# A DRAM scratch for rotated queries and keys, laid out row by row instead of block by block

## The chip, the core and the metric

The kernel runs on one core of one Trainium2 chip. The metric is device time in microseconds (us) of that core, the median of several runs. A core has five engines that each work through their own list of instructions: TensorE (PE, matmuls, with weight loads shown as PEld), VectorE (DVE), ScalarE (ACT), GpSimd (POOL) and SyncE (SP, which here only issues transfers). Transfers between DRAM and the on-chip buffers are issued by SP and by ACT and are carried out by 16 DMA engines.

## The reference, cut to what matters

One decoder layer on 1024 positions and width 2048: RMS norm, one input projection to 6144 columns, then differential attention with eight heads beside a gated linear recurrence with eight blocks, a gate on each, one output projection, residual and a final norm. The part that the change touches is the scores of the attention:

```python
q = rope(q.reshape(bsz, seq, N_ATTN_HEADS, 2, QK_DIM), cos, sin)   # QK_DIM = 64
k = rope(k.reshape(bsz, seq, N_ATTN_HEADS, 2, QK_DIM), cos, sin)
...
s = jnp.einsum('bhmqd,bhmkd->bhmqk', qb, kb).astype(jnp.float32) * scale
mask = jnp.arange(end)[None, :] <= (s0 + jnp.arange(Q_BLOCK))[:, None]
p = jax.nn.softmax(jnp.where(mask, s, -jnp.inf), axis=-1)
w = p[:, :, 0] - lam * p[:, :, 1]
```

Each head has two score maps (m = 0, 1) with 64 query and 64 key channels each; rope turns the first 32 channels against the second 32.

## The kernel before, in words

Work goes in two passes over the sequence, `b` = 0 and 1, of 512 positions each. A pass has sixteen units in the order of the table `UNITS`: eight heads (four projections of 128 columns each) and eight recurrent blocks (two projections each). Then `outputs(b)` computes the output projection of these positions. A projection (`project`, its matmuls in `triple`, L368) is 48 matmuls of 512 columns: 16 blocks of 128 input rows, each as three products, because every operand is split in two parts of fewer bits, "hi" and "lo" (`split`, L170 the ACT cast to hi, L171 the subtraction to lo). The weights are streamed: SP loads 128x512 pieces (`load`, L156, which issues every SP load), ACT casts them, POOL subtracts, and TensorE uses them.

The order of instructions on every engine is fixed when the kernel is built. A scheduler of "slots" (`Slots`) advances by one tick with nearly every triple of matmuls. Side tasks (rope, values, recurrence, loading a head, scores, softmax weights, head output) are generators that `yield` a number of ticks, and each one's instructions stand in the lists of the engines where their tick falls. An engine waits at each instruction until the data are there. The tile framework hands out eight DMA semaphores, named DMAHW0 to DMAHW7 below, in turn to the transfers of both issuing engines, and a transfer whose turn comes waits until the last one on its semaphore has landed, where that isn't known yet.

The path that the change touches, for each head and pass:

- `head` multiplies the two q/k projections by cos and sin (DVE, L174). The 128 rows of each are four groups of 32: query m=0, query m=1, key m=0, key m=1. The first projection has the first 32 channels, the second the other 32.
- `rope` adds and subtracts, and splits the two results into four tiles of 128x512: `t2` and `t4` (hi of the first and of the second half), `t1` and `t3` (lo of both). ACT then stores the four tiles to the DRAM scratch `fs` (L471).
- `head_load` brings them back on SP in the form that the score matmuls need: for each m a key tile of 128 rows (hi first, hi second, lo first, lo second: 4 blocks of 32 rows), a query tile with the 64 hi rows twice, and one with the 64 lo rows twice. In the second pass the key tiles and values of the first pass are loaded as well (eight transfers from `fs` and two from `vs`). The loader starts a head once its stores were issued six ticks before.
- `score` runs at least 24 ticks (pass 0) or 28 ticks (pass 1) after the loads: L634 multiplies the first query tile with the key tile, L635 adds the product of the second query tile.
- `values` stores the value tiles of pass 0 to `vs` on ACT (L493), and `head_out` writes the head's output, with L723 on ACT and the matmuls L726 and L737.

Of the kernel before, what the change touches and what calls it, by code (L numbers as in the profile page):

```python
# [13 lines left out]
F32 = mybir.dt.float32  # L14
# [11 lines left out]
HALF = 512  # L26
# [81 lines left out]
class Trunk:  # L108
# [351 lines left out]
    def rope(self, b, h, ts):  # L460
        nc = self.nc
        t1, t2, t3, t4 = ts
        self.tt(t1.f, t1.f, t2.f, ALU.subtract)
        self.tt(t3.f, t3.f, t4.f, ALU.add)
        yield 1
        self.split(t1.f, t2, t1)
        self.split(t3.f, t4, t3)
        yield 4
        fs = self.dram.tile([4, 4, 32, HALF], F32, name=self.nm("fs"))
        for i, t in enumerate((t2, t4, t1, t3)):  # L470
            nc.scalar.dma_start(fs[:, i], t.f)  # L471
        self.rel(*ts)
        self.fs[h, b] = fs
        yield 6
        self.ready.add(("q", h, b))
# [109 lines left out]
    def head_load(self, h, l):  # L585
        k, q, v = [], [], []
        for c in range(l + 1):
            ks = []
            for m in range(2):
                kk = self.allocr()  # L590
                self.load(kk.f, self.fs[h, c][2 + m].rearrange("i r c -> (i r) c"))
                ks.append(kk)
            k.append(ks)
        for i in (0, 2):
            for m in range(2):
                t = self.allocr()
                src = self.fs[h, l][m, i:i + 2].rearrange("i r c -> (i r) c")
                self.load(t.f, src.unsqueeze(0).broadcast_to([2, 64, HALF]))
                q.append(t)
        if l:  # L600
            vs = []
            for d in self.vsc[h]:
                t = self.allocr()
                self.load(t.f, d)
                vs.append(t)
            v.append(vs)
        self.hd[h, l] = (k, q, v)
        self.loaded[h, l] = self.sl.now
# [331 lines left out]
```

## Time and profile before

| what | value |
|---|---|
| time, median of 3 runs | 2099.34 us (2096.14 to 2101.21) |
| the profiled execution's own time | 2100.45 us |
| its span, first to last instruction | 2098.7 us |
| TensorE busy | 1724.3 us, 82% of the span |
| ACT, POOL and DVE busy | 38%, 40% and 37% |
| mean granted TensorE clock | 0.913 of full speed |
| moved by DMA | 237.02 MB, mean 113 GB/s |

TensorE is the busiest engine by far, so what counts is where it stands still and where it runs at the lower of its two clocks. A matmul of 512 columns takes about 0.23 us at the full clock; the durations in the profile also hold the time in which a matmul stands in the pipeline behind another one.

### The profile page before, as it was taken

Reading aid. Unit: us, or ns where it says so; the run is one execution under the profiler, and the core shown is the slowest. Engines: PE = TensorE matmul, PEld = TensorE weight load, DVE = VectorE, ACT = ScalarE, POOL = GpSimd, SP = SyncE. Lnnn points to the kernel's source line nnn. Section 1 sums busy time; section 2 is a strip of 40 time slices with the busy share of each in tenths; the row PEclk is TensorE's granted clock in tenths of the full one; section 3 lists DMA queues with packets and bytes.
Section 4 is the critical chain, followed back from the end, with each engine's and each line's share of the span. In section 5 each row is a group of like instructions: output and inputs, shape, how many; then the busy total and the mean of one; then the engine's idle time right before and its main releaser. Section 6 shows DMA issues by size and latency. Waiting matters only on the chain.

```text
span 2098.7 us, 22044 instructions
## 1 busy us (share of the span) xinstructions
PE 1724.3 (82%) x7716; PEld 1408.4 (67%) x7716; DVE 779.1 (37%) x1333; ACT 804.7 (38%) x1393; POOL 849.8 (40%) x710
## 2 busy tenths in 40 slices
PE   7758868787786779989979787878787879799996
PEld 5646756566665667768867576767676767587885
DVE  8515342414151325741115242424252515265101
ACT  6215242525161236633414342525252424365321
POOL 7313433434342325765632242424233333266560
PEclk9879989898898889999989898989898999899998
DMA  5432333333323235423652242323233232255312
GB/s 209 135 112 74 109 97 110 94 105 93 120 79 120 79 98 170 159 81 99 214 185 84 79 119 81 113 90 113 91 106 97 90 115 83 89 181 188 113 63 80
DMA packets 131502, 237.02 MB, mean 113 GB/s; under 512 B 13248, under 2 KB 17472, under 8 KB 131392
## 3 DMA queue, kind: packets, MB, share of 16 engines
q1 hardware_dynamic: 116032, 206.27, 31.6%
q10 hardware_dynamic: 15360, 29.36, 4.0%
q8 instruction: 60, 0.98, 0.2%
q14 instruction: 50, 0.41, 0.1%
HBM read 197.83 MB, written 37.75 MB: 112 GB/s over the span
## 4 chain that ended last, share of the span: by engine, by line
PE 31%; DMA 14%; DVE 7%; ACT 3%; issue 2%; SPq 2%; POOL 1%; ACTq 0%; POOLq 0%; DVEq 0%
PE pq L368 11%; PE pq L829 8%; PE sw L829 8%; DMA fs<-b 5%; DMA b<-fs 4%; DMA b<-w_in 4%; SPq L156 2%; DVE b L174 2%; DMA ms<-b 1%; PE pq L758 1%; DVE sw L639 1%; ACT wide L646 1%; DVE b L533 1%; ACT b L170 1%; DVE wide L654 1%
## 5 line engine op out<-in xcount | busy, mean ns | idle before, releaser
L368 PE MATMUL pq<-b,b 128*128 128x512 f32 x4512 | 1151.6, 408 | 83.7 <-DVE b L171 64.0
L171 POOL TENSOR_TENSOR b<-b,b 128x512 fp32r<-128x512 f32 x504 | 671.9, 1347 | 1033.0 <-ACT b L170 720.8
L368 PEld LDWEIGHTS pq<-b,b 128*128 128x128 f32 x4512 | 871.5, 198 | 263.9 <-DVE b L171 67.8
L170 ACT CAST b<-b 128x512 fp32r<-128x512 f32 x592 | 349.2, 617 | 962.2 <-DMA b<-w_in 390.5
L829 PE MATMUL pq<-b,b 128*128 128x512 f32 x768 | 197.6, 393 | 4.4 <-DVE wide L174 4.4
L829 PE MATMUL sw<-b,b 128*128 128x512 f32 x768 | 197.0, 392 | 0.0
L174 DVE TENSOR_TENSOR b<-pq,b 128x512 f32<-128x512 f32 x113 | 74.8, 686 | 276.6 <-PE pq L368 180.9
L829 PEld LDWEIGHTS pq<-b,b 128*128 128x128 f32 x768 | 144.8, 189 | 35.8 <-DVE wide L174 4.8
L829 PEld LDWEIGHTS sw<-b,b 128*128 128x128 f32 x768 | 145.6, 190 | 30.6
L174 POOL TENSOR_TENSOR b<-b,b 128x512 f32<-128x512 f32 (+1 forms) x98 | 126.4, 1291 | 65.2 <-DVE b L740 29.0
L635 PE MATMUL sw<-b,b 128*128 128x512 f32 (+2 forms) x192 | 70.7, 377 | 83.8 <-DMA b<-fs 83.8
L646 ACT ACTIVATE wide<-sw,mx 128x128 f32<-128x128 f32 (+7 forms) x128 | 93.9, 737 | 88.0 <-DVE mx L642 50.1
L639 DVE CUSTOM_DVE_ANT_0 sw<-sw,mask 128x128 f32<-128x128 f32 (+7 forms) x128 | 95.2, 774 | 79.6 <-PE sw L635 79.6
L758 PE MATMUL pq<-ident,wide 128*128 128x128 f32 x288 | 56.0, 304 | 66.9 <-DVE wide L654 63.2
L634 PE MATMUL sw<-b,b 128*128 128x512 f32 (+2 forms) x192 | 69.4, 367 | 40.5 <-DMA b<-fs 33.2
L635 PEld LDWEIGHTS sw<-b,b 128*128 128x128 f32 x192 | 38.4, 200 | 94.3 <-DMA b<-fs 88.9
L171 DVE TENSOR_TENSOR b<-b,b 128x512 fp32r<-128x512 f32 x88 | 88.9, 1033 | 29.3 <-ACT b L170 26.0
L455 DVE SCALAR_TENSOR_TENSOR b<-b,b 128x512 f32<-128x512 f32 x32 | 31.1, 971 | 178.0 <-ACT b L453 178.0
L758 PEld LDWEIGHTS pq<-ident,wide 128*128 128x128 f32 x288 | 38.0, 154 | 85.9 <-DVE wide L654 73.0
L768 DVE TENSOR_TENSOR b<-pq,b 128x512 fp32r<-128x512 f32 (+1 forms) x80 | 50.9, 636 | 103.6 <-ACT b L767 96.7
L767 ACT CAST b<-pq 128x512 fp32r<-128x512 f32 (+1 forms) x80 | 43.2, 540 | 99.3 <-PE pq L758 89.7
L634 PEld LDWEIGHTS sw<-b,b 128*128 128x128 f32 x192 | 38.2, 199 | 49.2 <-issue 30.3
(130 smaller groups left out, 1345.8 us busy)
## 6 DMA issues: line engine op xcount, KB each, us to landing
b<-w_in SPq DMA_DIRECT2D x384, 256.0 KB
b<-w_out SPq DMA_DIRECT2D x128, 256.0 KB
b<-fs SPq DMA_DIRECT2D x112, 256.0 KB
fs<-b ACTq DMA_DIRECT2D x64, 256.0 KB
b<-xt SPq DMA_DIRECT2D x32, 256.0 KB
ms<-b ACTq DMA_DIRECT2D x32, 256.0 KB
b<-ms SPq DMA_DIRECT2D x32, 256.0 KB
wide<-x SPq DMA_DIRECT2D x20, 256.0 KB
```

Source lines behind the costliest of these rows:

```text
L170: self.nc.scalar.copy(hi.r, x)
L171: (eng or self.nc.vector).tensor_tensor(out=lo.r, in0=x, in1=hi.f, op=ALU.subtract)
L174: (eng or self.nc.vector).tensor_tensor(out=out, in0=a, in1=b, op=op)
L368: self.nc.tensor.matmul(acc, lhsT=x.r[:, s], rhs=y.r, start=kt == 0 and j == 0, stop=kt == KT - 1 and j == 2)
L634: nc.tensor.matmul(o, lhsT=q[m].r[:, qs], rhs=kk, start=True, stop=False)
L635: nc.tensor.matmul(o, lhsT=q[2 + m].r[:, qs], rhs=kk, start=False, stop=True)
L639: nc.vector.tensor_tensor_reduce(out=s, in0=s, in1=self.mask[:, 896 - off:896 - off + cols], scale=1.0, scalar=NEG, op0=ALU.add, op1=ALU.m ...
L646: nc.scalar.activation(p[:, :cols], self.swide[m][:, :cols], AF.Exp, scale=QK ** -0.5, bias=mx[:, m:m + 1], accum_out=sm[:, m:m + 1])
L758: nc.tensor.transpose(self.tr[:, c:c + P], ws[qi][:, kb * P:(kb + 1) * P], self.ident)
L767: nc.scalar.copy(wh.r[:, first:], self.tr[:, first:])
L768: nc.vector.tensor_tensor(out=wl.r[:, first:], in0=self.tr[:, first:], in1=wh.f[:, first:], op=ALU.subtract)
L829: nc.tensor.matmul(accs[t], lhsT=x.r[:, s], rhs=z.r, start=i == 0 and j == 0, stop=i == KT - 1 and j == 2)
```

## The change

The scratch `fs` of a head gets another layout. Before it was group, block, row: for each of the four groups of 32 rows, four blocks (hi first, hi second, lo first, lo second) of 32 rows, 64 KB each. Now it is group, row, block: each of the 128 rows has six places side by side, 2 KB each, for hi first, hi second, lo first, lo second, hi first, hi second. Two more stores of 64 rows fill places 4 and 5 for the query groups. A key tile is places 0 to 3 of 32 rows. The two query tiles are places 0 to 3 and places 2 to 5 of 32 rows: the first now multiplies hi with hi and lo with lo, the second lo with hi and hi with lo, which sum to the same four products.

```diff
-        fs = self.dram.tile([4, 4, 32, HALF], F32, name=self.nm("fs"))
+        fs = self.dram.tile([4, 32, 6, HALF], F32, name=self.nm("fs"))
         for i, t in enumerate((t2, t4, t1, t3)):
-            nc.scalar.dma_start(fs[:, i], t.f)
+            nc.scalar.dma_start(fs[:, :, i].rearrange("g r c -> (g r) c"), t.f)
+        for i, t in enumerate((t2, t4)):
+            nc.scalar.dma_start(fs[:2, :, 4 + i].rearrange("g r c -> (g r) c"), t.f[:64])
         self.rel(*ts)
...
                 kk = self.allocr()
-                self.load(kk.f, self.fs[h, c][2 + m].rearrange("i r c -> (i r) c"))
+                self.load(kk.f, self.fs[h, c][2 + m, :, :4])
...
         for i in (0, 2):
             for m in range(2):
                 t = self.allocr()
-                src = self.fs[h, l][m, i:i + 2].rearrange("i r c -> (i r) c")
-                self.load(t.f, src.unsqueeze(0).broadcast_to([2, 64, HALF]))
+                self.load(t.f, self.fs[h, l][m, :, i:i + 4])
                 q.append(t)
```

On ACT, at the third head of pass 0, the list holds these rows (fs is the scratch, b are tiles of 128x512, and the size is that of the side that is written; in brackets the semaphores waited for). Before:

```order
L170 CAST b_1377<-b_1376 128x512 [waits DVE_49]
L471 DMA fs_1637<-b_1375 4x32x512 [waits Activation_49]
L471 DMA fs_1637<-b_1377 4x32x512 [waits DMAHW4_49,Activation_49]
L471 DMA fs_1637<-b_1374 4x32x512 [waits DMAHW5_49,DVE_49]
L471 DMA fs_1637<-b_1376 4x32x512 [waits DMAHW7_49,DVE_49]
L170 CAST b_1867<-b_1741 128x512 [waits DMAHW4_49]
```

And in the changed kernel at the same place:

```order
L170 CAST b_1381<-b_1380 128x512 [waits DVE_49]
L471 DMA fs_1641<-b_1379 128x512 [waits Activation_49]
L471 DMA fs_1641<-b_1381 128x512 [waits DMAHW0_49,Activation_49]
L471 DMA fs_1641<-b_1378 128x512 [waits DMAHW1_49,DVE_49]
L471 DMA fs_1641<-b_1380 128x512 [waits DMAHW3_49,DVE_49]
L473 DMA fs_1641<-b_1379 64x512 [waits DMAHW4_49]
L473 DMA fs_1641<-b_1381 64x512 [waits DMAHW5_49]
L170 CAST b_1851<-b_1716 128x512 [waits DMAHW1_49]
```

The written side of a store was four groups of 32 rows and is now one run of 128 rows, and the two stores of 64 rows stand ahead of the next cast of a weight piece.

On SP the same head is loaded by these rows. Before (b_1675 and b_1677 are the hi queries, b_1671 and b_1673 the keys, b_1679 and b_1681 the lo queries):

```order
L156 DMA b_1874<-w_in 128x512 [waits DMAHW6_49,PE_49]
L156 DMA b_1675<-fs_1637 128x1x512 [waits DMAHW4_49,DMAHW3_49]
L156 DMA b_1677<-fs_1637 128x1x512 [waits DMAHW1_49]
L156 DMA b_1671<-fs_1637 128x512 [waits DMAHW7_49,DMAHW5_49,DMAHW2_49]
L156 DMA b_1673<-fs_1637 128x512
L156 DMA b_1679<-fs_1637 128x1x512
L156 DMA b_1681<-fs_1637 128x1x512
L156 DMA b_1852<-w_in 128x512 [waits DMAHW6_49,DVE_49]
```

And in the changed kernel (b_1677 and b_1679 are the keys, the other four the queries):

```order
L156 DMA b_1880<-w_in 128x512 [waits DMAHW2_49,PE_49]
L156 DMA b_1677<-fs_1641 128x1x512 [waits DMAHW6_49,DMAHW3_49,DMAHW7_49,DMAHW1_49,DMAHW0_49]
L156 DMA b_1679<-fs_1641 128x1x512
L156 DMA b_1681<-fs_1641 128x1x512
L156 DMA b_1683<-fs_1641 128x1x512
L156 DMA b_1685<-fs_1641 128x1x512 [waits DMAHW5_49,DMAHW4_49,DMAHW2_49]
L156 DMA b_1687<-fs_1641 128x1x512
L156 DMA b_1858<-w_in 128x512 [waits DVE_49]
```

The six loads keep their place between two weight loads; the keys now stand first, the first load waits for all four large stores instead of two, and the last two loads wait for the two new stores.

## Rows read from the trace of the kernel before

**Rows 1.** The page's first part, busy time, share of the span and instructions, and its slices of the granted TensorE clock.

```profile
PE 1724.3 (82%) x7716; PEld 1408.4 (67%) x7716; DVE 779.1 (37%) x1333; ACT 804.7 (38%) x1393; POOL 849.8 (40%) x710
PEclk9879989898898889999989898989898999899998
```

**Rows 2.** Who TensorE waited for over the whole span: line, releaser, us in total, times, longest.

```profile
PE sw L635 <- DMA b<-fs: 83.8, 17, 9.3
PE pq L368 <- DVE b L171: 64.0, 7, 12.3
PE pq L758 <- DVE wide L654: 63.2, 22, 5.4
PE pq L726 <- ACT b L723: 44.1, 3, 14.8
...
PE sw L634 <- DMA b<-fs: 33.2, 6, 8.8
...
PE pq L737 <- DVE hs L734: 8.7, 2, 7.8
...
PE sw L634 <- ACT wide L646: 7.2, 1, 7.2
```

**Rows 3.** TensorE in order of time around the first scores of a head of pass 0: start, duration, what, and in brackets the idle time before and its releaser.

```profile
349.10 11.85 PE L368 MATMUL pq<-b,b 128*128 128x512 f32 x51
365.13 0.55 PE L634 MATMUL sw<-b,b 128*128 128x256 f32 x1 [4.18 <-DMA b<-fs]
372.81 0.58 PE L635 MATMUL sw<-b,b 128*128 128x256 f32 x1 [7.13 <-DMA b<-fs]
...
377.96 0.58 PE L635 MATMUL sw<-b,b 128*128 128x256 f32 x1 [4.36 <-DMA b<-fs]
378.34 8.58 PE L368 MATMUL pq<-b,b 128*128 128x512 f32 x30
```

**Rows 4.** ACT in order of time around the same head; ACTq is its sequencer, which issues transfers.

```profile
338.60 0.53 ACTq L471 DMA_DIRECT2D fs<-b  x1
...
339.69 2.74 ACTq L471 DMA_DIRECT2D fs<-b  x3
348.40 0.62 ACT L170 CAST b<-b 128x512 fp32r<-128x512 f32 x1 [8.75 <-DMA fs<-b]
350.97 0.62 ACT L170 CAST b<-b 128x512 fp32r<-128x512 f32 x1 [1.94 <-DMA fs<-b]
...
378.63 1.14 ACT L170 CAST b<-b 128x512 fp32r<-128x512 f32 x2 [25.73 <-DMA b<-w_in]
```

**Rows 5.** SP's issues in order of time around the same head (a merged row lasts from the first issue to the end of the last).

```profile
341.45 0.33 SPq L156 DMA_DIRECT2D b<-w_in  x1
348.45 13.91 SPq L156 DMA_DIRECT2D b<-fs  x6
```

**Rows 6.** The chain that ended last, in order of time, around a head of pass 1.

```profile
1364.94 10.80 DMA fs<-b
...
1375.82 4.38 SPq L156
...
1382.01 20.58 DMA b<-fs
```

**Rows 7.** TensorE in order of time around the same head of pass 1.

```profile
1372.91 9.12 PE L368 MATMUL pq<-b,b 128*128 128x512 f32 x39
1392.03 7.34 PE L368 MATMUL pq<-b,b 128*128 128x512 f32 x24 [10.00 <-DVE b L171]
...
1402.63 0.80 PE L635 MATMUL sw<-b,b 128*128 128x512 f32 x1 [2.35 <-DMA b<-fs]
...
1403.65 7.97 PE L368 MATMUL pq<-b,b 128*128 128x512 f32 x30
```

**Rows 8.** ACT in order of time around the same head of pass 1.

```profile
1390.15 0.62 ACT L170 CAST b<-b 128x512 fp32r<-128x512 f32 x1 [17.33 <-DMA b<-w_in]
```

**Rows 9.** Two stretches of pass 1 in which transfers of fs alone are under way: the stretch, its length, busy time (and instructions) of PE, PEld, DVE, ACT and POOL, granted clock, mean busy share of the 16 DMA engines, GB/s.

```profile
1366.50:1373.00 6.50, 6.50 (x33) 5.39 (x32) 0.69 (x1) 2.56 (x5) 2.44 (x2) 1.00 0.25 88
1384.50:1388.50 4.00, 0.00 (x0) 0.00 (x0) 0.00 (x0) 0.00 (x0) 0.00 (x0) 0.59 0.13 50
```

**Rows 10.** DMA queues (q10 is ACT's: packets, MB, share of 16 engines' span) and the issues of ACT and those of fs on SP (number, KB each).

```profile
q10 hardware_dynamic: 15360, 29.36, 4.0%
...
b<-fs SPq DMA_DIRECT2D x112, 256.0 KB
fs<-b ACTq DMA_DIRECT2D x64, 256.0 KB
...
ms<-b ACTq DMA_DIRECT2D x32, 256.0 KB
...
vs<-b ACTq DMA_DIRECT2D x16, 256.0 KB
```

**Rows 11.** Two other transfers of 256 KB on the chain that ended last: a store of a 128x512 tile on ACT (pass 1) and a load of a 128x512 weight piece on SP.

```profile
1329.29 4.88 DMA ms<-b
...
1847.41 2.78 DMA b<-w_out
```

**Rows 12.** What SP's own queue waited for over the whole span.

```profile
SPq L156 <- PE pq L368: 355.2, 112, 20.8
...
SPq L156 <- DMA fs<-b: 187.8, 34, 10.4
```

## The prediction, made before the changed kernel was run

> **What bounds the kernel now.** I read the page's first part, then TensorE's waits, then one head in each pass in order of time on TensorE, ACT and SP. TensorE is busy for 82% of the span, no other engine for more than 40% [rows 1], so time is won only where TensorE stands still or is slowed. Its list of waits [rows 2] is led by the scratch: L635 and L634 wait 83.8 and 33.2 us for loads of fs. L368 "for DVE L171" (64.0 us) and L726 "for ACT L723" (44.1 us) don't name fs, so their cause has to be found.
>
> In pass 0 [rows 3], TensorE runs out at 349.10 + 11.85 = 360.95 us and then waits 4.18, 7.13 and 4.36 us, all for fs: 15.7 us in one head. ACT issued the four stores at 338.60 to 342.4 [rows 4]. Two casts that need the stored tiles' buffers go at 348.40 and 350.97: the stores land one by one, 2.6 us apart. The last queries release L635 at 372.81 and 377.96, so the query loads land 5.15 us apart. SP issues nothing but fs from 348.45 to 362.4 [rows 5], so weight loads are held as well, and ACT waits 25.73 us for one of them [rows 4].
>
> In pass 1 the same trip is on the chain that ended last [rows 6]: 10.80 us for a store, SP from 1375.82 on, 20.58 us for a load. TensorE stops at 1382.03 for 10.00 us [rows 7]. The releaser named is a DVE subtraction, but it needs ACT's cast, and ACT stood for 17.33 us behind a weight load in its own order [rows 8]. So these waits of L368 are the fs trip as well, by way of a weight piece that was stuck behind it. L726 waits for an ACT instruction that stands in the same place (three of about 15 us). Behind that L635 still waits 2.35 us for fs.
>
> **Why the trip is slow.** While stores of fs alone are under way, a quarter of the 16 DMA engines is busy and 88 GB/s move; while query loads alone are under way, 0.13 of them and 50 GB/s, with every compute engine idle [rows 9]. That is 4 engines and 2. The counts agree for the stores: ACT's queue has 15360 packets for 64 + 32 + 16 = 112 transfers of 128 rows each; the 1024 beyond 112 x 128 are 48 x 16 + 64 x 4, if each engine that takes part sends one more packet at its end [rows 10]. Four and two are the outermost sizes on the DRAM side before: a store writes [4 groups, 32 rows], a query load reads [2 copies, 64 rows]. An engine thus moves 64 KB in 2.6 us and 128 KB in 5.15 us, about 25 GB/s in either case; on 16 engines 256 KB would take 2.6/4 = 0.65 us of engine time.
>
> The Trainium skill, "DMA: Bandwidth & Descriptors", section "Why a DMA increments its semaphore by 16 and not by 1", states that a copy uses the largest number of engines, at most 16, that divides the slowest non-unit dimension of both sides. The trace agrees with 4 and 2. By that rule the new transfers (128, 64 and 32 outermost) run on 16, which gives the same sum as below.
>
> **The change part by part.**
>
> *Stores.* Four of 128 rows now have 128 outermost. I price them by the row of the same size and issuer with 128 rows outermost: ms<-b took 4.88 us on the chain [rows 11], with other traffic around it, against 10.80 for fs. Bounds: 2.78 us (the weight load [rows 11]) and 10.80 (nothing gained). I take 4.9.
>
> *Two more stores per head*, 32 in all, 4.2 MB. Issue costs ACT 0.53 us each in the first row of [rows 4], 32 x 0.53 = 17 us on an engine that is busy 38%; in pass 0 they end before the cast of 348.40, which now waits for the stores. On the DMA engines half a tile costs 0.33 us. At nothing; without cover, 1 us per head, 17 us. A rows-apart store (2 KB every 12 KB) isn't in the trace; between nothing and the 4.9 already taken I leave it at that.
>
> *Six loads per head* (four from the head's own scratch in both passes and two keys, plus two old keys in pass 1). Before, four query loads held two DMA engines for 4 x 5.15 = 20.6 us, just the 20.58 of [rows 6]. No row has 32 outermost; 4 gave 4 engines, 2 gave 2 and 128 gave 16, so I take 16: 0.65 us each, 6 x 0.65 = 3.9 us, behind an issue of 0.53 us each as for a store. Bounds: 3.9, and 20.6 if nothing changes.
>
> *The new wait.* The first load waits for all four stores, the fifth for the two extra ones, and the weight loads behind them on SP wait too. That costs what the last store is later than the second: in pass 0 the last is issued by 342.4, the extra ones by 343.5, so all have landed by 343.5 + 4.9 = 348.4, no later than the first query load was issued before (348.45) [rows 5]. So it costs nothing against before.
>
> *What arrives when.* Pass 0: 348.4 + 6 x 0.53 of issue + 3.9 + 2.8 (a lone load) = 358.3 at the latest, before TensorE asks at 360.95. The 15.7 us go. Pass 1: the store on the chain is issued at 1364.94, the last three follow within 2 us, so they land by about 1371.9; the loads are issued by 1375.1 and the next weight piece lands 2.8 + 3.9 us behind, at 1381.8, when TensorE would stop (1382.03). A slip of 1 or 2 us can remain of 10.00, but all terms are upper ones: 4.88 and 2.78 already hold the waiting that I add again.
>
> *Sum.* Waits on fs 83.8 + 33.2, L368 64.0, L726 44.1: 225.1 us. I add the waits of L737 (8.7) and of L634 for ACT (7.2), single waits in which ACT stood behind the same transfers: 241.0. After a stop TensorE runs at the lower clock for a while (0.59 granted in the second row of [rows 9]): 30 matmuls in 8.58 us against 51 in 11.85, 0.054 us more each, 1.6 us [rows 3]; in pass 1 by the same comparison 24 x 0.073 + 30 x 0.033 = 2.8 us [rows 7]. Six stops in pass 0 (L634's count) and three of L726 at 1.6, six in pass 1 at 2.8: 31 us. Together 272 us. 2098.7 - 272 = 1826.7; around the span lie 1.75 us, and the median of the runs is 1.1 us under the profiled one: **1827 us**.
>
> What is late next is not the scratch: L758 waits for the softmax weights 22 times, 63.2 us in all [rows 2], and that stays.
>
> **The rivals.**
>
> *Only four engines per load.* If the smaller of [32 rows, 4 blocks] counted, each load would take 2.6 us, keys included: 15.6 us per head. In pass 0 the loads would end at 348.4 + 2.8 + 15.6 = 366.8, a wait of about 5 us, six times; in pass 1 the weight piece would come at 1371.9 + 2.8 + 15.6 = 1390.3, so 8 of the 10 us stay, six times, and about 10 of 15 us of L726 three times: 30 + 48 + 30 = 108 us less gain, 1935 us. For it: 4 and 2 are also the smaller sizes in the old shapes. Against it: nothing in these rows but the stores of 4 x 32 and the loads of 2 x 64, which fit both. Chance 0.08.
>
> *The next wait takes the place.* TensorE's pauses gave ACT, DVE and POOL time to catch up. If L758's waits double (63.2) and each brings its stretch of low clock (22 x 1 us), the time is 1827 + 85 = 1912; if half of L368's stay too (32), 1944. For it: L758 waits in both passes. Against it: no engine beside TensorE is over 40% busy. Chance 0.12.
>
> *Slower.* Stores five and six wait for DMA semaphores whose last user can be a weight load that SP itself holds back for a buffer; ACT would stand there, its casts with it, and TensorE after them. SP's longest wait for TensorE is 20.8 us [rows 12]. Held that long in each of 16 heads it is 333 us: 1827 + 333 = 2160. It decides from 272/16 = 17 us per head on. Against it: before, three stores were issued in 2.74 us [rows 4], the last of them two semaphores short of where the sixth is now. Chance 0.03.
>
> *No change.* If the DRAM side and not the number of engines limits these transfers, or the weights would have stopped TensorE in any case, it stays at 2099. The second row of [rows 9] speaks against it: nothing else is at work. Chance 0.02.
>
> **How the numbers follow.** The forecast itself has 0.75. Its own range is 1784 to 1865: 43 us below if half of L758's waits go with the rest (32, and 11 slow stretches of 1 us), 38 above if 2.4 us remain in each of 16 heads. The range for 8 in 10 takes in the first rival and the first form of the second: 1784 to 1940. A difference of 0.2% is about what a measurement of this kernel can tell. Faster: 0.75 + 0.08 + 0.12 = 0.95; same 0.02; slower 0.03.
>
> **What would show it.** Right: no wait of L634 or L635 on fs above 1 or 2 us; L368's waits on DVE L171 in pass 1 and L726's three gone; ACT's waits for weight pieces shorter; fs trips on the chain of about 5 and 7 us; ACT's queue (q10) with 64 x 144 + 32 x 80 + 48 x 144 = 18688 packets; a higher mean clock. Wrong: stores or loads still some 2.6 us apart (engines), L758 or weight waits grown (next wait), ACT idle ahead of the casts behind the stores (slower).

## The result, and the profile of the changed kernel

| | before | changed |
|---|---|---|
| median of four runs each, side by side | 2097.74 us | 1792.55 us (1791.60 to 1793.18) |
| span of the profiled execution | 2098.7 us | 1791.4 us |
| TensorE busy | 1724.3 us | 1670.4 us |
| TensorE idle (span less busy) | 374.4 us | 121.0 us |
| mean granted TensorE clock | 0.913 | 0.970 |

The ratio is 0.8548, with a 95% interval of 0.8525 to 0.8572: 305 us less. The forecast was 1827 us with a range of 1784 to 1940. In the spans the gain is 307.3 us: 253.4 us of idle time and 53.9 us in which the same matmuls were done faster. Line numbers behind the diff have grown by 1 or 2: the score matmuls are L635 and L636 now, the transposes L759.

The page of the changed kernel, busy time by engine, the slices of the granted clock, and the DMA queues of SP and ACT; they answer to [rows 1, 10]:

```profile
PE 1670.4 (93%) x7716; PEld 1375.7 (77%) x7716; DVE 774.1 (43%) x1333; ACT 808.4 (45%) x1393; POOL 850.8 (47%) x710
PEclk9899999999999999899999999999999999999998
q1 hardware_dynamic: 116928, 206.27, 37.0%
q10 hardware_dynamic: 18688, 33.56, 5.2%
```

TensorE has the same number of matmuls and is now busy for 93% of the span. ACT's queue (q10) has the 18688 packets that were worked out for 16 engines per store. SP's queue (q1) tells the same of the loads: it has 812 transfers, and 116928 is 812 x (128 + 16), one packet per row and 16 more for each transfer, so the 112 loads of fs run on 16 engines as well. Before it had 116032, which is 748 x (128 + 16) + 64 x (128 + 2): the 64 query loads on two engines, all others on 16. The same way of counting fits both queues in every run below.

Issues of the changed kernel, with the median us from issue to landing:

```profile
b<-fs SPq DMA_DIRECT2D x112, 256.0 KB, 4.5
fs<-b ACTq DMA_DIRECT2D x64, 256.0 KB, 3.3
ms<-b ACTq DMA_DIRECT2D x32, 256.0 KB, 3.1
```

A store of fs now takes 3.3 us and a load 4.5 us, where the chain before had 10.80 and 20.58 [rows 6].

Who TensorE waits for in the changed kernel, to be read against [rows 2]:

```profile
PE pq L759 <- DVE wide L655: 55.4, 21, 5.0
...
PE pq L368 <- DVE b L171: 1.4, 1, 1.4
...
PE pq L738 <- DVE hs L735: 0.9, 1, 0.9
```

The two lines of the score matmuls are gone from the list, and so is the wait behind the head's output (L726 before). The waits of L368 that had added up to 64.0 us are 1.4 us. The transposes' wait for the softmax weights is on top.

One head of pass 0 in order of time on TensorE, the place of [rows 3]:

```profile
283.46 11.85 PE L368 MATMUL pq<-b,b 128*128 128x512 f32 x51
295.15 0.28 PE L635 MATMUL sw<-b,b 128*128 128x256 f32 x1
...
295.62 6.99 PE L368 MATMUL pq<-b,b 128*128 128x512 f32 x30
```

The same 51 matmuls take the same 11.85 us, and the scores follow at once. The 30 matmuls behind them take 6.99 us in place of 8.58.

ACT and then SP around that head, the places of [rows 4] and [rows 5]:

```profile
274.05 2.62 ACTq L471 DMA_DIRECT2D fs<-b  x3
276.70 1.13 ACTq L473 DMA_DIRECT2D fs<-b  x2
278.40 0.62 ACT L170 CAST b<-b 128x512 fp32r<-128x512 f32 x1 [4.39 <-DMA fs<-b]
...
280.63 0.62 ACT L170 CAST b<-b 128x512 fp32r<-128x512 f32 x1 [1.30 <-DMA fs<-b]
```

```profile
275.81 0.33 SPq L156 DMA_DIRECT2D b<-w_in  x1
279.73 3.76 SPq L156 DMA_DIRECT2D b<-fs  x6
283.53 13.14 SPq L156 DMA_DIRECT2D b<-w_in  x5
```

SP issues the six loads in 3.76 us (13.91 before) and goes on to weights at 283.53, 7.7 us after the last weight load ahead of them; before it was 21 us (341.45 to 362.4). With 4.5 us to landing the last load, issued by 283.5, is there at about 288, some 7 us before TensorE asks.

In pass 1, at the head of [rows 7], TensorE runs through:

```profile
1154.04 14.57 PE L368 MATMUL pq<-b,b 128*128 128x512 f32 x63
1168.45 0.39 PE L635 MATMUL sw<-b,b 128*128 128x512 f32 x1
```

These 63 matmuls are the 39 and the 24 between which there were 10.00 us. Two stretches around the loads of these heads, read like [rows 9]:

```profile
279.00:290.00 11.00, 11.00 (x52) 9.09 (x51) 1.39 (x2) 2.20 (x6) 5.38 (x6) 1.00 0.84 255
1150.00:1162.00 12.00, 12.00 (x56) 9.92 (x56) 1.38 (x2) 3.62 (x7) 7.27 (x6) 1.00 0.76 239
```

The DMA engines are 0.84 and 0.76 busy, at 255 and 239 GB/s, where it was 0.25 and 0.13 with 88 and 50 GB/s, and TensorE is never idle. Weight loads are under way in these stretches too, so they show that the loads of fs no longer hold the others up, not their own rate.

### The profile page after: what moved, and what is told of

It is laid out like the page before. It is cut to its first block, busy times and chain, and to the rows that moved or that the text cites. A ratio compares the mean times of both kernels' runs of the same rounds, so it can differ in the third digit from the quotient of the medians.

```text
span 1791.4 us, 22085 instructions
## 1 busy us (share of the span) xinstructions
PE 1670.4 (93%) x7716; PEld 1375.7 (77%) x7716; DVE 774.1 (43%) x1333; ACT 808.4 (45%) x1393; POOL 850.8 (47%) x710
## 3 DMA queue, kind: packets, MB, share of 16 engines
q1 hardware_dynamic: 116928, 206.27, 37.0%
q10 hardware_dynamic: 18688, 33.56, 5.2%
## 5 line engine op out<-in xcount | busy, mean ns | idle before, releaser
L368 PE MATMUL pq<-b,b 128*128 128x512 f32 x4512 | 1114.6, 399 | 19.0 <-DVE b L174 9.5
L368 PEld LDWEIGHTS pq<-b,b 128*128 128x128 f32 x4512 | 846.0, 191 | 188.3 <-DVE b L174 9.9
L830 PE MATMUL pq<-b,b 128*128 128x512 f32 x768 | 198.8, 394 | 4.3 <-DVE wide L174 4.3
L830 PE MATMUL sw<-b,b 128*128 128x512 f32 x768 | 197.2, 392 | 0.0
L830 PEld LDWEIGHTS pq<-b,b 128*128 128x128 f32 x768 | 145.7, 190 | 36.6 <-DVE wide L174 4.8
L830 PEld LDWEIGHTS sw<-b,b 128*128 128x128 f32 x768 | 145.8, 190 | 30.6
L759 PE MATMUL pq<-ident,wide 128*128 128x128 f32 x288 | 56.1, 305 | 56.6 <-DVE wide L655 55.4
L759 PEld LDWEIGHTS pq<-ident,wide 128*128 128x128 f32 x288 | 38.0, 155 | 74.5 <-DVE wide L655 65.1
L769 DVE TENSOR_TENSOR b<-pq,b 128x512 fp32r<-128x512 f32 (+1 forms) x80 | 50.9, 636 | 92.1 <-ACT b L768 87.0
L174 DVE TENSOR_TENSOR wide<-pq,wide 128x512 f32<-128x512 f32 x12 | 8.2, 690 | 167.8 <-PE pq L830 167.8
L635 PE MATMUL sw<-b,b 128*128 128x512 f32 (+2 forms) x192 | 65.2, 347 | 0.0
L636 PE MATMUL sw<-b,b 128*128 128x512 f32 (+2 forms) x192 | 64.3, 346 | 0.0
L650 DVE TENSOR_TENSOR es<-sm 128x1 f32<-128x1 f32 x64 | 27.6, 432 | 76.9 <-ACT wide L647 76.3
L767 POOL MEMSET b<- 128x128 f32 x64 | 12.7, 205 | 89.1 <-PE pq L368 26.1
```

Of the source, the lines that this page charges most:

```text
L174: (eng or self.nc.vector).tensor_tensor(out=out, in0=a, in1=b, op=op)
L368: self.nc.tensor.matmul(acc, lhsT=x.r[:, s], rhs=y.r, start=kt == 0 and j == 0, stop=kt == KT - 1 and j == 2)
L635: nc.tensor.matmul(o, lhsT=q[m].r[:, qs], rhs=kk, start=True, stop=False)
L636: nc.tensor.matmul(o, lhsT=q[2 + m].r[:, qs], rhs=kk, start=False, stop=True)
L759: nc.tensor.transpose(self.tr[:, c:c + P], ws[qi][:, kb * P:(kb + 1) * P], self.ident)
L769: nc.vector.tensor_tensor(out=wl.r[:, first:], in0=self.tr[:, first:], in1=wh.f[:, first:], op=ALU.subtract)
```

## The experiments

The theory: what mattered is how many DMA engines carry a transfer, and the loads are the larger half of it. The rivals: the stores alone were what made the trip slow; the new layout (8 KB runs) and not the number of engines helps; the extra stores or the larger number of transfers cost something that is hidden in the gain. Each diff below is against the changed kernel, unless it says otherwise. A transfer is called narrow when two or four engines carry it, because the outermost size on its DRAM side is 2 or 4, and wide when all 16 do.

| kernel | median, us | span | TensorE busy | idle |
|---|---|---|---|---|
| changed | 1792.55 | 1791.4 | 1670.4 | 121.0 |
| e1, all stores narrow | 1896.27 | 1890.2 | 1693.0 | 197.2 |
| e9, large stores narrow, extra ones wide | 1869.38 | 1865.1 | 1684.3 | 180.8 |
| e5, the kernel before with wide query loads | 1847.20 | 1840.5 | 1681.4 | 159.1 |
| e3, loads on four engines | 1930.19 | 1925.0 | 1707.7 | 217.3 |
| e2, queries on two engines | 2001.12 | 1998.2 | 1719.4 | 278.8 |
| before | 2097.74 | 2098.7 | 1724.3 | 374.4 |

**Narrow stores (e1).**

```diff
-        fs = self.dram.tile([4, 32, 6, HALF], F32, name=self.nm("fs"))
+        fs = self.dram.tile([4, 33, 6, HALF], F32, name=self.nm("fs"))
         for i, t in enumerate((t2, t4, t1, t3)):
-            nc.scalar.dma_start(fs[:, :, i].rearrange("g r c -> (g r) c"), t.f)
+            nc.scalar.dma_start(fs[:, :32, i], t.f)
         for i, t in enumerate((t2, t4)):
-            nc.scalar.dma_start(fs[:2, :, 4 + i].rearrange("g r c -> (g r) c"), t.f[:64])
+            nc.scalar.dma_start(fs[:2, :32, 4 + i], t.f[:64])
...
-                self.load(kk.f, self.fs[h, c][2 + m, :, :4])
+                self.load(kk.f, self.fs[h, c][2 + m, :32, :4])
...
-                self.load(t.f, self.fs[h, l][m, :, i:i + 4])
+                self.load(t.f, self.fs[h, l][m, :32, i:i + 4])
```

> The changed kernel with one empty row between the groups of the scratch (33 rows for 32), so that a store's DRAM side is four groups of 32 rows again (two for the extra stores), while the loads stay 32 rows of four places. Theory (the number of DMA engines per transfer sets the length of the trip, and the loads are the larger half): stores land 2.6 us apart again, the loads stay short. In pass 0 the last load lands at about 294.5 us on the clock of the changed kernel's trace against the 295.15 at which TensorE asks, so nothing is lost there; in pass 1 SP is held some 16 us and the next weight piece comes about 8 us late, six times. About 1793 + 50 = 1845 us. Rival (the stores are what made the trip slow): most of the 305 us come back, 2000 us or more. Second rival (nothing in the widths: it is the layout, 8 KB runs on the load side): as the changed kernel, 1793.

Measured: 1896.27 us, ratio to before 0.9045 (0.8994 to 0.9097). It is between the theory and the rivals: 104 us of the gain go with the stores, twice what was expected, but two thirds stay. The loads of TensorE's scores are in time, as expected (waits of 3.4 and 1.3 us for fs in the whole run). What was missed is ACT. In order of time in pass 1:

```profile
1123.15 2.88 ACTq L471 DMA_DIRECT2D fs<-b  x4
1126.07 6.56 ACTq L473 DMA_DIRECT2D fs<-b  x2
1132.72 1.14 ACT L170 CAST b<-b 128x512 fp32r<-128x512 f32 x2 [9.01 <-DMA fs<-b]
```

The two extra stores, two outermost, take 6.56 us to issue behind the four large ones, and then the casts of weight pieces wait for the stores, because they write into buffers that held the stored tiles. ACT's wait for stores over the whole run, in e1 and then in the changed kernel:

```profile
ACT b L170 <- DMA fs<-b: 219.1, 24, 16.6
```

```profile
ACT b L170 <- DMA fs<-b: 61.7, 23, 7.8
```

And TensorE in e1 waits 31.8 us in L368 (1.4 in the changed kernel) and 82.5 us for the softmax weights (55.4), which pass over the same ACT. That ACT's wait for the stores is what makes these two longer is argued from its place in the order, not tried apart:

```profile
PE pq L759 <- DVE wide L655: 82.5, 23, 7.8
PE pq L368 <- DVE b L171: 31.8, 10, 5.1
```

**Narrow large stores, wide extra ones (e9)**, formed to see what the extra stores' share of that is. Against e1:

```diff
         for i, t in enumerate((t2, t4)):
-            nc.scalar.dma_start(fs[:2, :32, 4 + i], t.f[:64])
+            for g in range(2):
+                nc.scalar.dma_start(fs[g, :32, 4 + i], t.f[32 * g:32 * g + 32])
```

> As the run with narrow stores (padded groups, the four large stores on four engines), but each extra store is written as two stores of 32 rows, one per group, which are 32 outermost and so wide. Theory formed from that run (1896 us where 1845 was expected): its extra stores, two outermost and so on two engines, stood behind the large ones for another 5 us, and ACT's casts that take the stored tiles' buffers stood with them; without that the time is near that of the kernel before with wide query loads (1847 us), 1850. Rival (the padding or the number of stores costs): 1890 us or more.

Measured: 1869.38 us, ratio 0.8918 (0.8884 to 0.8952). The width of the extra stores is worth some 27 us of the 104 (it takes four stores of 32 rows in place of two of 64). The rest isn't down to 1850: ACT's wait for stores is still 178.3 us.

```profile
ACT b L170 <- DMA fs<-b: 178.3, 24, 17.5
```

Wide or not, the extra stores are issued behind the narrow ones, and the casts wait for both. How the remaining 77 us divide between the large stores, the extra ones behind them and the empty row between the groups, this run doesn't tell; e5 below puts some 55 us to large narrow stores with nothing behind them.

**Narrow query loads (e2).** The scores are of other data than they should be; the amount of work is the same.

```diff
-                self.load(t.f, self.fs[h, l][m, :, i:i + 4])
+                src = self.fs[h, l][m].rearrange("r i c -> (r i) c")[64 * (i // 2):64 * (i // 2) + 64]
+                self.load(t.f, src.unsqueeze(0).broadcast_to([2, 64, HALF]))
```

> The changed kernel with the query loads in their old shape, 64 neighbouring places of 2 KB read twice (two outermost), while stores and key loads stay wide. These places are not the rows that the scores need, so the scores are of other data; the amount of work is the same. Theory (widths, loads the larger half): each query load takes 5.15 us on two engines, four of them 20.6 us. Pass 0: the last lands some 8 us after TensorE asks, six times; pass 1: the next weight piece is some 10 us late, six times; the three waits behind the head's output about 10 us each; with the lower clock after the stops 1793 + 160 = 1955 us. Rival (stores): about 1793 to 1810. A DMA busy share of 0.13 must come back in stretches where only query loads are under way.

Measured: 2001.12 us, ratio 0.9545 (0.9518 to 0.9573): 209 us of the gain go with the query loads, 46 more than expected. A stretch in which TensorE waits for queries, and TensorE's waits for the queries (L637 in this kernel) and for a late weight piece (L368):

```profile
349.00:352.00 3.00, 0.00 (x0) 0.00 (x0) 0.00 (x0) 0.00 (x0) 0.00 (x0) 1.00 0.13 51
```

```profile
PE sw L637 <- DMA b<-fs: 105.3, 24, 8.3
...
PE pq L368 <- DVE b L171: 0.6, 1, 0.6
```

Two of the 16 engines are busy again (0.13, 51 GB/s), with stores and keys wide and the layout new. So it is not the layout as such. One head in pass 0:

```profile
355.60 0.58 PE L637 MATMUL sw<-b,b 128*128 128x256 f32 x1 [7.30 <-DMA b<-fs]
...
360.73 0.58 PE L637 MATMUL sw<-b,b 128*128 128x256 f32 x1 [4.33 <-DMA b<-fs]
361.11 9.71 PE L368 MATMUL pq<-b,b 128*128 128x512 f32 x30
```

The wait is 11.6 us where 8 were expected, and the 30 matmuls behind it take 9.71 us against 6.99 in the changed kernel. In pass 1 the expectation had the wrong place: L368 waits 0.6 us for weight pieces in the whole run and not some 10 us in each of six heads; TensorE waits for the queries themselves there too, two waits of 1.7 to 4.7 us in each of six heads. The time of e2 thus bears out the price of narrow query loads, not the path that was forecast for pass 1.

**All loads on four engines (e3).** Also on other data, with the same amount of work.

```diff
-                self.load(kk.f, self.fs[h, c][2 + m, :, :4])
+                src = self.fs[h, c][m].rearrange("r i c -> (r i) c")[64:64 + 32]
+                self.load(kk.f, src.unsqueeze(0).broadcast_to([4, 32, HALF]))
...
-                self.load(t.f, self.fs[h, l][m, :, i:i + 4])
+                src = self.fs[h, l][m].rearrange("r i c -> (r i) c")[32 * i:32 * i + 32]
+                self.load(t.f, src.unsqueeze(0).broadcast_to([4, 32, HALF]))
```

> The changed kernel with all loads from the scratch as 32 neighbouring places read four times (four outermost); the stores stay wide. The scores are of other data than needed, with the same amount of work. This measures the first rival of the prediction, four engines per load, which was priced at 1935 us by upper terms. Theory with the times of the changed kernel's trace: a load takes 2.6 us, six 15.6 us; TensorE waits about 3 us per head in pass 0, weights come about 5 us late per head in pass 1: 1793 + 80 = 1870 us. If the time were simply proportional to the width (four engines between two and sixteen), it would lie near 1900 or above.

Measured: 1930.19 us, ratio 0.9207 (0.9166 to 0.9248). The prediction's first rival had 1935 for this case. That the two are so near is luck: the rival had 30 us of waits for loads and 78 us behind weight pieces and the head's output, and the run has 62.1 us for loads, 0.2 us of L368 for a weight piece and 8.9 us behind the head's output. The expectation above, which used shorter times, was 60 us too low: it counted 80 us, and idle time grew by 96 us and the matmuls took 37 us more. SP's queue in this run has 812 x 128 + 700 x 16 + 112 x 4 = 115584 packets, four engines for each of the 112 loads:

```profile
q1 hardware_dynamic: 115584, 206.26, 34.6%
```

TensorE's two longest waits in it, and the two of which the rival had expected most:

```profile
PE pq L761 <- DVE wide L657: 70.9, 22, 7.7
PE sw L638 <- DMA b<-fs: 62.1, 25, 5.5
...
PE pq L729 <- ACT b L726: 8.9, 2, 4.9
...
PE pq L368 <- DVE b L171: 0.2, 1, 0.2
```

**The kernel before with wide query loads (e5).** Against the kernel before; layout and stores are untouched.

```diff
                 src = self.fs[h, l][m, i:i + 2].rearrange("i r c -> (i r) c")
-                self.load(t.f, src.unsqueeze(0).broadcast_to([2, 64, HALF]))
+                for p in (0, 64):
+                    self.load(t.f[p:p + 64], src)
```

> The kernel before, layout and stores unchanged (four groups of 32 rows, narrow), with each query load written as two loads of 64 rows into 64 partitions instead of one with two copies outermost; the reads are wide, and SP issues ten transfers per head in place of six. Theory (widths): nearly all of the gain without the new layout; the stores still take 10.4 us in a row, so pass 1 loses about 4 us per head against the changed kernel: about 1825 us. Rival (stores are the slow half): little gain, 2050 us or more. Rival (the issue of more transfers on SP and the shared DMA semaphores costs): 1900 us or more.

Measured: 1847.20 us, ratio 0.8811 (0.8754 to 0.8869): 250 of the 305 us without a new layout, by taking the outermost 2 off the query loads. The 55 us that are left are put down to narrow stores with wide loads and no store behind them; the layout and the number of transfers differ from the changed kernel too, but e8 below, with more loads and no extra stores, shows that these cost nothing that can be told.

**The extra stores twice (e4), and none at all (e8).**

```diff
-        fs = self.dram.tile([4, 32, 6, HALF], F32, name=self.nm("fs"))
+        fs = self.dram.tile([4, 32, 8, HALF], F32, name=self.nm("fs"))
...
-        for i, t in enumerate((t2, t4)):
+        for i, t in enumerate((t2, t4, t2, t4)):
             nc.scalar.dma_start(fs[:2, :, 4 + i].rearrange("g r c -> (g r) c"), t.f[:64])
```

> The changed kernel with eight places per row and the two extra stores written twice (places 4 to 7), so each head has eight stores in place of six. Theory (the extra stores are covered): ACT issues two more transfers per head, about 1.1 us, SP's first query loads wait about 1 us longer, and TensorE asks 6.6 us after the loads have landed in pass 0: 1793 us, at most 1800. Rival (the slower case of the prediction, stores on ACT wait for shared DMA semaphores and hold the casts behind them): 1.1 us or more per head reach TensorE, 1810 us or more.

Measured: 1796.24 us (1793.44 to 1797.00), ratio 0.8571 (0.8555 to 0.8587). That is 3.7 us over the changed kernel, and the intervals overlap: two more wide stores per head cost a few us or nothing.

```diff
-        fs = self.dram.tile([4, 32, 6, HALF], F32, name=self.nm("fs"))
+        fs = self.dram.tile([4, 32, 4, HALF], F32, name=self.nm("fs"))
...
-        for i, t in enumerate((t2, t4)):
-            nc.scalar.dma_start(fs[:2, :, 4 + i].rearrange("g r c -> (g r) c"), t.f[:64])
...
-                self.load(kk.f, self.fs[h, c][2 + m, :, :4])
+                for i in (0, 2):
+                    self.load(kk.f[32 * i:32 * i + 64], self.fs[h, c][2 + m, :, i:i + 2])
...
-                self.load(t.f, self.fs[h, l][m, :, i:i + 4])
+                for p in (0, 64):
+                    self.load(t.f[p:p + 64], self.fs[h, l][m, :, i:i + 2])
```

> The row layout with four places and no extra stores; every key and query tile is loaded by two transfers of 64 partitions (32 rows of two neighbouring places), so SP issues twelve per head in place of six, all 32 outermost. Theory (width is what counts, the count of transfers is covered): the same as the changed kernel within 10 us, 1793. Rival (SP's issue and the eight shared DMA semaphores): twelve issues of 0.6 us, of which the ninth must wait for the first to land, take some 4 us more per head and hold the next weight piece: 1830 us or more.

Measured: 1794.54 us (1790.50 to 1794.98), ratio 0.8566 (0.8548 to 0.8584): no difference from the changed kernel that can be told. Four places and twice as many loads do as well as six places and two extra stores. Wide loads of half the size land sooner, after 2.9 us in place of 4.5:

```profile
b<-fs SPq DMA_DIRECT2D x224, 128.0 KB, 2.9
```

**What is late next (e6, e7).** The mark that lets a score block be transposed is set four ticks later (e6), or four and eight (e7, pass 0 and pass 1).

```diff
                     yield from self.score(h, l, j, p0, es)
-                    self.scored.append(p0)
                     yield SCORE_PACE[l]
+                    self.scored.append(p0)
```

> The changed kernel with the four ticks that follow a score block moved ahead of the mark that the block is ready for transposing. The longest wait that is left, the transposes (L759) for the softmax weights of DVE, 55.4 us in 21 waits, is one of a chain that hasn't finished when TensorE reaches it; four ticks are about 2.8 us of matmuls. Theory: the waits of pass 0 (1.1 and 3.3 us) go nearly, those of pass 1 (5.1 us) fall to about 2.3: 30 us less wait and 6 us less slow clock, 1757 us. Rival (the chain is held by ACT, whose place in the order moves too): same as the changed kernel, 1793 us.

```diff
                     yield from self.score(h, l, j, p0, es)
+                    yield (4, 8)[l]
                     self.scored.append(p0)
-                    yield SCORE_PACE[l]
```

> As the run before with eight ticks in pass 1 (four more than before, so a score block takes 14 ticks there in place of 10). Theory: the waits of pass 1 go too, about 1745 us. Rival: the longer block holds the p0 buffers and the next head longer, and the gain goes back: 1780 us or more.

Measured: e6 1765.38 us, ratio 0.8427 (0.8411 to 0.8442); e7 1761.15 us, ratio 0.8405 (0.8390 to 0.8420). Both beat both kernels, and both fall short of their expectation, by 8 and 16 us. The 4 us between them are not told from nothing by the intervals. TensorE's waits in e6, then in e7:

```profile
PE pq L759 <- DVE wide L655: 24.7, 12, 4.8
...
PE pq L759 <- DVE b L769: 9.6, 8, 1.7
```

```profile
PE pq L759 <- DVE wide L655: 21.1, 6, 4.7
...
PE pq L759 <- DVE b L769: 10.7, 13, 1.4
```

The wait for the softmax weights falls from 55.4 to 24.7 and 21.1 us, in 12 and 6 places. The transposes now wait for DVE's subtraction of the piece before (L769) for some 10 us, 1.3 in the changed kernel (three waits of at most 0.5). Waits of up to 4.7 us remain with eight ticks as well; what holds these was not tried.

## Why the prediction was right, and which term was off

- **The cause of the trip.** Four engines per store and two per query load, taken from the busy share of the DMA engines and the packet counts, holds: e1 and e2 each bring part of the lost time back (104 and 209 us) by the outermost size, and e5 takes 250 us off the kernel before by it. The packets of e1 count the same way: 112 x 128 + 32 x 64 rows and 64 x 4 + 32 x 2 + 48 x 16 at the ends are 17472, which its page has. One agreement in the prediction is partly chance: the 20.58 us of [rows 6] are not four query loads but the last of them alone, from its issue at 1382.01 to its landing, with weight pieces under way beside it.

```profile
q10 hardware_dynamic: 17472, 33.56, 4.9%
```

- **That 32 outermost means 16 engines** rested on the rows for 4, 2 and 128. The 116928 packets of SP's queue show it, and the load times of 4.5 us fit; four engines measure 1930 us. By the rule of the Trainium skill, "DMA: Bandwidth & Descriptors", section "Why a DMA increments its semaphore by 16 and not by 1", the slowest dimension decides and not the smallest; the changed kernel, with [32 rows, 4 places] and 16 packets more per load, agrees.
- **L368 and L726 as the trip's own waits.** Right. 241.0 us of waits were counted; 2.3 of them are left (1.4 of L368, 0.9 of L738). The slip of 1 or 2 us per head in pass 1 didn't come: the stores took 3.3 us where 4.9 were taken, and waiting had been added twice, as the text allowed.
- **Nothing lost by the new wait and the extra stores.** Right: SP's wait for stores fell from 187.8 us [rows 12] to 55.6, and e4 and e8 show the price of the extra stores as nothing that can be told. But the reason given was too narrow. What the stores hold is not SP and the scores alone but ACT, through the casts that take the stored tiles' buffers: 219.1 us in e1, where narrow extra stores stand behind narrow large ones. Without extra stores it is less, 90.3 us before and 78.4 us in e5, against 61.7 us in the changed kernel, so what e1 shows on ACT is for the most part not what the kernel before lost. The lines are SP's wait in the changed kernel, and ACT's before and in e5:

```profile
SPq L156 <- DMA fs<-b: 55.6, 24, 6.2
```

```profile
ACT b L170 <- DMA fs<-b: 90.3, 16, 19.1
```

```profile
ACT b L170 <- DMA fs<-b: 78.4, 17, 9.8
```

- **The term that was mis-sized: the slower clock after a stop.** The sum had 31 us for it; TensorE's busy time fell by 53.9 us. The step that failed is the count of the matmuls affected: it took one or two rows of L368 behind each stop. L368 as a whole fell from 1151.6 to 1114.6 us, 37.0, and the score matmuls themselves, which stand at the stop and run slowly, from 70.7 + 69.4 to 65.2 + 64.3 us, 10.6 more; some 6 us are in other lines. The lines of after for L635 and L636:

```profile
L635 PE MATMUL sw<-b,b 128*128 128x512 f32 (+2 forms) x192 | 65.2, 347 | 0.0
L636 PE MATMUL sw<-b,b 128*128 128x512 f32 (+2 forms) x192 | 64.3, 346 | 0.0
```

  That it is the clock can be read from the stretches of the span that were granted the lower clock. Their sums (length, then busy time of each engine), before and after:

```profile
sum 365.27, PE 164.47 PEld 131.94 DVE 71.83 ACT 88.80 POOL 81.10; mean PE 4.33 PEld 3.47 DVE 1.89 ACT 2.34 POOL 2.13
```

```profile
sum 106.60, PE 72.48 PEld 57.66 DVE 54.64 ACT 42.70 POOL 39.53; mean PE 4.26 PEld 3.39 DVE 3.21 ACT 2.51 POOL 2.33
```

  TensorE was busy at the lower clock for 164.5 us before and for 72.5 us after. Eight matmuls take 3.45 us in one such stretch before (1385.24 to 1395.48), 0.43 us each against 0.23, so about half of the 92 us between the two are lost: an estimate of 46 of the 53.9 us. The rest is open.

- **What lay beside.** The other 14.7 us of idle time come from waits that were not counted: L758's went from 63.2 to 55.4 us instead of staying, and several small ones shrank. 253.4 + 53.9 = 307.3 us against 272: 12 us from waits (14.7 more, 2.3 left) and 23 from the slower matmuls. The time is in the range, 34 us under the forecast, but not for the reason that the range gave for its low end: that half of L758's waits, 32 us, would go. They fell by 7.8 us.
- **The rivals.** The next wait did not take the place: no wait grew. The slower case did not come, with eight stores per head either. "No change" fell with the first run. "Only four engines" is ruled out by SP's packet count.

## What to carry to other kernels

Look at the outermost size on the DRAM side of every transfer that something waits for: a copy count or a handful of groups there makes a short transfer long, and everything behind it on the same queue with it, even at a mean DMA load of a third. A view of the DMA engines' busy share in a stretch where one kind of transfer is alone shows it in one row. It may take no new layout: here two half loads in place of one broadcast gave 250 of the 305 us.

A wait that names a compute engine can belong to a transfer: follow that engine's own order back to what it stood behind. And a stop of TensorE costs more than its length: in these runs, against the changed kernel, each us of added idle time came with 0.2 to 0.4 us of slower matmuls (e1 22.6 for 76.2, e2 49.0 for 157.8, e3 37.3 for 96.3, e5 11.0 for 38.1, e9 13.9 for 59.8, before 53.9 for 253.4).

## What the runs showed of the hardware that was not expected

- Issues that stand behind several narrow transfers are held. At the head of [rows 7] SP issues the first two query loads of the kernel before in 1.16 us, but the last takes 6.20 us and the wide weight load behind it 5.01 us, and in e1 two small stores behind four narrow ones took ACT 6.56 us (1.13 us for the two in the changed kernel). Six loads took SP 3.76 us when wide; the 13.91 us before [rows 5] hold a wait of some 5 us for the stores as well.

```profile
1373.25 1.16 SPq L156 DMA_DIRECT2D b<-fs  x2
...
1382.01 6.20 SPq L156 DMA_DIRECT2D b<-fs  x1
1388.25 5.01 SPq L156 DMA_DIRECT2D b<-w_in  x1
```

- Rows of 2 KB written 12 KB apart cost nothing that can be seen: 3.3 us from issue to landing against 3.1 us for ms<-b, whose rows lie side by side.
- Narrow stores and narrow loads cost more together than apart. Narrow query loads cost 209 us beside wide stores (e2 against the changed kernel) and 250 us beside narrow ones (before against e5). Narrow stores with nothing behind them cost some 55 us beside wide loads (e5), so 55 + 209 = 264 of the 305 us, and some 41 come only when both are narrow. The 104 us of e1 are not the price of the stores of the kernel before, because e1 has two narrow extra stores per head that it doesn't have. Why the two don't add was not tried.
